# Prompt attention of a hybrid decoder step: one visit for each unit instead of two, with its pace, its query blocks and its compressed scores moved

## The chip, the core and the metric

The kernel runs on one core of one Trainium2 chip. The metric is the device time of one execution in microseconds (us). TensorE is PE in what follows (PEld is its weight load, which runs beside the matmuls), VectorE is DVE, ScalarE is ACT, GpSimd is POOL, SyncE is SP. Each engine takes its instructions in the order in which the program writes them.

## What is computed

One layer of a decoder for two groups of requests that share the weights: 256 prompt tokens and 8 x 8 sample tokens, 320 columns together.

```python
x = x + 0.5 * swiglu_ffn(rmsnorm(x, ffn1_norm), ffn1_w_in, ffn1_w_out)
h = rmsnorm(x, mix_norm)
z, xbc, dt_raw, q, kv, nsa_g, merge_g = jnp.split(h @ w_in_proj, cuts, axis=-1)
y_ssm, new_conv, new_ssm = mamba_mixer(z, xbc, dt_raw, ...)     # conv, chunked scan, gated norm
o, new_win = nsa_fn(q, gates, paged_rows, win_rows, compress_kv, bias_tab)
mix = (gm[..., :D_MODEL] * (y_ssm @ w_branch_ssm) + gm[..., D_MODEL:] * (o @ w_branch_attn)) @ w_out
x = x + mix
x = x + 0.5 * swiglu_ffn(rmsnorm(x, ffn2_norm), ffn2_w_in, ffn2_w_out)
```

`nsa_fn` is attention in three branches for every head: compressed (one key for each 32 tokens), selected blocks, and a sliding window, each with a softmax of its own; the three are added with a sigmoid gate each. For the prompt, 256 tokens have only four selectable blocks, so that the selected branch and the window branch are both plain causal attention with their own keys and values.

## The kernel before, in words

**The dense stream.** All weights go through `dense` (L328 to L354). A weight block of 128x1024 is split into a high and a low part (`wh` on ACT, L317; `wl` on DVE, L326), and each of its eight slices makes three matmuls over the 320 columns, L345, L346 and L347. These three are called a k-tile here. There are 1928 of them in the program, and they are written in a fixed order: first feed-forward, input projection (q, k, v, then 24 tiles of `xbc`, each with a short convolution, `conv_unit`), merge gates, z, two branch outputs, output, second feed-forward.

**The work beside it.** Everything else is written as Python generators that the class `Sched` steps through. After each k-tile `S.tick()` adds half of `S.rate` to a credit, and for each whole credit one generator goes on to its next `yield`. What it issues up to there, on whatever engine, stands in the program between two k-tiles. Such a step is called a visit. Two generators in the queue take turns. `RATE` holds the rates of the stages, and `pace(i)` sets them: `RATE[3]` is that of the prompt attention. At 1.5 there are 0.75 visits for each k-tile.

**Prompt attention** (`prompt_attn`) has 32 units: four query blocks `qc` of 64 tokens, and in each of them eight units `u` (two heads on 128 partitions). Beside it, taking turns, runs the chain `values_tok`, `new_keys`, `cmp_sample` (the sample tokens' compressed branch), and then that chain is done. A unit goes through

- `scores` (L1317 on PE into a bank of tag `sc`, sum with bias and minimum on DVE L1323, exponential on ACT L1326),
- `norm` (reciprocal on DVE L1334, scaling on POOL L1337),
- `transposes` (L1349 on PE into a bank of tag `pt`, copied to `pT` by ACT L1350),
- `values` (L1366 on PE into the bank `po`, of which there is one; after the eighth unit ACT copies it out, L1370).

Once in a query block, `build` writes the next block of queries (POOL L1281), `cmp_a` computes its compressed scores (L1288 on PE, nine small DVE instructions and one of ACT), and `cmp_b` turns them (L1310 on PE into `pt` banks, copied by ACT L1311). Tags `sc` and `pt` have two PSUM banks each, shared with the other chain.

The convolution's tanh (L1246) is on ACT between these, and waits for three DVE instructions (L1245). `conv_unit` puts them off by four k-tiles.

Of the kernel before, what the change touches and what calls it, by code (L numbers as in the profile page):

```python
# [112 lines left out]
W0, W1, W2, W3, WS, EB = 3, 3, 6, 1, 4, 2  # L113
XBC_RUN = [i for q in range(4) for i in (4 * q, 4 * q + 1, 4 * q + 2, 4 * q + 3, 16 + q, 20 + q)]
PROJ_RUN = [12] + list(range(12)) + [17, 18, 19, 20, 13, 14, 15, 16] + [PROJ_X + i for i in XBC_RUN] + [PROJ_M + i for i in range(16)] + [PROJ_Z + i for i in range(16)]
RATE = (0.59, 1.2, 0.9, 1.5, 0.88, 0.57, 1.0)


IDLE = "idle"
# [48 lines left out]
def chain(*gens):  # L168
    for x in gens:
        yield from x  # L170
# [21 lines left out]
def wait(n):  # L192
    for _ in range(n):
        yield
# [3 lines left out]
def step_kernel(ctx, tc, I, O):  # L198
    nc = tc.nc
    pe, v, a, g, sp = nc.tensor, nc.vector, nc.scalar, nc.gpsimd, nc.sync  # L200
# [10 lines left out]
    def bank(tag, shape=(128, 512)):  # L211
        bufs = dict(pd=3, sc=2, pt=2, po=1)[tag]
        t = ps.tile([128, 512], F32, tag=tag, bufs=bufs, name=f"ps_{tag}")[: shape[0], : int(np.prod(shape[1:]))]
        if len(shape) == 3:
            t = t.rearrange("p (a b) -> p a b", a=shape[1])
        elif len(shape) == 4:
            t = t.rearrange("p (a b c) -> p a b c", a=shape[1], b=shape[2])
        return t
# [4 lines left out]
    pt = cp.tile([1, 128], I32, name="pt")  # L223
# [16 lines left out]
    def flat(t):  # L240
        return t.rearrange("p a b -> p (a b)")
# [562 lines left out]
    S.add(cs)  # L804
    S.rate = RATE[0]
    sq = Squares(8)
# [43 lines left out]
    kTp = pp.tile([128, 2, 8], F32, name="kTp")  # L850
# [17 lines left out]
    def bl(o, m, n):  # L868
        return st["blob"][:, o : o + m * n].rearrange("p (a b) -> p a b", a=m)
# [25 lines left out]
    def selector():  # L895
        st["sel"] = pa.tile([128, 12, 128], F32R, name="sel")
        id4 = ident.rearrange("p (x r) -> p x r", x=4)
        for k in range(3):
            gcopy(st["sel"][:, 4 * k : 4 * k + 4, :].rearrange("p x (h d) -> p x h d", h=2),
                  id4[:, :, 2 * k : 2 * k + 2].unsqueeze(3).to_broadcast([128, 4, 2, 64]))  # L900
            yield
# [128 lines left out]

    def values_tok():
        for t in range(2):
            pv = bank("pt")
            for i in range(4):
                pe.transpose(pv[:, 128 * i : 128 * i + 128], vr[:, i, 128 * t : 128 * t + 128], ident)
            a.copy(flat(vtp[:, t]), pv)
            yield
        pv = bank("pt", (128, 256))
        for br in range(2):
            for h2 in range(2):  # L1040
                pe.matmul(pv[64 * br : 64 * br + 64, 128 * h2 : 128 * h2 + 128], vr[:, 2 * br + h2, 256:], ident,
                          start=True, stop=True)
        a.copy(vst, pv)
        yield
# [216 lines left out]
    def prompt_attn():  # L1261
# [3 lines left out]
        qbp = [bl(1024 * i, 8, 128) for i in range(2)]  # L1265
# [4 lines left out]
        def move():  # L1270
            if ready["prep"] and "OT" not in st:
                st["OT"] = hp_.tile([128, 8, NT], F32, tag="OT", name="OT")
            if moves and "OT" in st:
                t = moves.pop()
                a.copy(st["OT"][:, :, t], qn[:, :, t])


        def build(qc):
            for hp in range(2):
                r = slice(64 * hp, 64 * hp + 64)  # L1280
                g.tensor_scalar(qbp[qc % 2][r, :, 64 * hp : 64 * hp + 64], qn[r, 0:8, 64 * qc : 64 * qc + 64], -1.0, 0.0,  # L1281
                                op0=ALU.mult, op1=ALU.add)

        def cmp_a(qc):
            nb, k0 = 2 * (qc + 1), 192 - 64 * qc
            pc = bank("pt", (128, 8, 8))
            for u in range(8):
                pe.matmul(pc[:, u, :nb], qbp[qc % 2][:, u, :], kTp[:, u // 4, :nb], start=True, stop=True)  # L1288
            sc = pl.tile([128, 8, 8], F32, tag="psc", name="psc")
            m = pl.tile([128, 8], F32, tag="psm", name="psm")  # L1290
            s = sc[:, :, :nb]
            bcast = m.unsqueeze(2).to_broadcast([128, 8, nb])
            v.tensor_tensor(s, pc[:, :, :nb], pb[:, :, k0 + 31 :: 32], op=ALU.add)
            v.tensor_reduce(out=m, in_=s, axis=AX.X, op=ALU.min)
            v.tensor_scalar(m, m, 1e20, None, op0=ALU.min)
            v.tensor_tensor(s, s, bcast, op=ALU.subtract)
            a.activation(s, s, AF.Exp, scale=-1.0)
            v.reduce_sum(m, s, axis=AX.X)
            v.tensor_scalar(m, m, 1e-30, None, op0=ALU.max)
            v.reciprocal(m, m)  # L1300
            gq = gtp[:, qc].rearrange("p (u r) -> p u r", r=3)
            v.tensor_tensor(m, m, gq[:, :, 0], op=ALU.mult)
            v.tensor_tensor(s, s, bcast, op=ALU.mult)
            pend["c"] = sc

        def cmp_b(qc, q):
            nb, sc = 2 * (qc + 1), pend["c"]
            tps = bank("pt")
            for i in range(4):
                pe.transpose(tps[:nb, 128 * i : 128 * i + 128], sc[:, 4 * q + i, :nb], ident)  # L1310
            a.copy(flat(pcT[qc % 2][:nb, 4 * q : 4 * q + 4]), tps[:nb])  # L1311

        def scores(i):
            qc, u = divmod(i, 8)
            nk, k0 = 64 * (qc + 1), 192 - 64 * qc
            p = bank("sc", (128, 2, 256))
            pe.matmul(p[:, :, :nk], qbp[qc % 2][:, u, :], knp[:, :, u // 4, :nk], start=True, stop=True)  # L1317
            P = pl.tile([128, 2, 256], F32, tag="pS", bufs=4, name="pS")
            if nk % 128:
                g.memset(P[:, :, nk : nk + 64], 0.0)  # L1320
            m = pl.tile([128, 4], F32, tag="pm", bufs=6, name="pm")
            for br in range(2):
                v.tensor_tensor_reduce(out=P[:, br, :nk], in0=p[:, br, :nk], in1=pb[:, u, k0:256], op0=ALU.add,  # L1323
                                       op1=ALU.min, scale=1.0, scalar=3e38, accum_out=m[:, br : br + 1])
            for br in range(2):
                a.activation(P[:, br, :nk], P[:, br, :nk], AF.Exp, bias=m[:, br : br + 1], scale=-1.0,  # L1326
                             accum_out=m[:, 2 + br : 3 + br])
            pend["s", i] = P, m

        def norm(i):  # L1330
            qc, u = divmod(i, 8)
            nk = 64 * (qc + 1)
            P, m = pend["s", i]
            v.reciprocal(m[:, 2:4], m[:, 2:4])  # L1334
            for br in range(2):
                o = 3 * u + 1 + br
                g.tensor_scalar(P[:, br, :nk], P[:, br, :nk], m[:, 2 + br : 3 + br], gtp[:, qc, o : o + 1], op0=ALU.mult,  # L1337
                                op1=ALU.mult)


        def transposes(i):
            nt = (i // 8 + 2) // 2
            P = pend.pop(("s", i))[0]
            tps = bank("pt")
            pT = pl.tile([128, 4, 128], F32, tag="pT", bufs=2, name="pT")
            for k in range(nt):
                for br in range(2):
                    o = (k * 2 + br) * 128
                    pe.transpose(tps[:, o : o + 128], P[:, br, 128 * k : 128 * k + 128], ident)  # L1349
            a.copy(flat(pT[:, 0 : 2 * nt, :]), tps[:, 0 : 256 * nt])  # L1350
            pend["t", i] = pT
# [20 lines left out]
                    moves.append(slice(64 * qc, 64 * qc + 64))  # L1372

        build(0)
        yield from wait(2)
        cmp_a(0)
        yield from wait(4)
        cmp_b(0, 0)
        cmp_b(0, 1)
        for i in range(4):  # L1380
# [6 lines left out]
        for i in range(32):  # L1387
            qc, u = divmod(i, 8)
            if i + 3 < 32:
                norm(i + 3)  # L1390
            if i + 1 < 32:
                transposes(i + 1)
            if i + 4 < 32:
                scores(i + 4)
            yield
            values(i)
            move()
            if qc < 3:
                if u == 1:
                    build(qc + 1)  # L1400
                elif u == 2:
                    cmp_a(qc + 1)
                elif u == 4:
                    cmp_b(qc + 1, 0)
                    cmp_b(qc + 1, 1)
            yield
        pr_stack.close()
        yield from until("prep")
# [475 lines left out]
    def until(name):  # L1884
        while not ready[name]:
            yield IDLE

    ssq = bank("po", (128, NT))
    def pace(i):
        S.rate = RATE[i]  # L1890
        yield IDLE
# [9 lines left out]
    early = chain(cmp_keys(), bias_, selector(), until("gates"), both(gates_rows(), decays()))  # L1901
    S.rate = RATE[1]
    S.add(chain(early, until("qk"), pace(2), qk_norm(ssq), done("qn"), until("side"), attention()),
# [28 lines left out]
    for i in range(4):  # L1932
# [5 lines left out]
        c, h2 = divmod(i, 2)  # L1938
# [281 lines left out]
```

## Time and profile before

| | us |
|---|---|
| three runs | 1324.02, 1332.32, 1332.83; median 1332.32 |
| the profiled execution | 1327.57 |
| its span, first to last instruction | 1325.9 |
| PE busy in the span | 1262.7 (95%) |
| DVE, ACT, POOL busy | 877.8, 590.7, 372.7 |

The profiled execution is 4.7 us below the median of the three runs, so a difference worked out in the profile is taken from the median. PE's ends are modelled, and a busy PE is not PE at its peak. What a stage costs is read from when its k-tiles start, and from what PE waited for between them.

### The profile page before, as it was taken

The page shows a single profiled execution, that of the slowest core. Times are in us where ns is not written, and L with a number is a line of the kernel's source. Part 1 is how long each engine was busy: PE and PEld are TensorE (multiplying, and loading weights), DVE is VectorE, ACT ScalarE, POOL GpSimd, SP SyncE. Part 2 cuts the span into 40 slices and gives each one's busy share as a digit, 9 for nine tenths or more (in the row PEclk, how much of TensorE's full clock was granted, in tenths as well). Part 3 has the DMA queues.
Part 4 walks back from the last instruction along what each step waited for, and adds up shares of the span by engine and source line. Part 5 has one row for each costly group of instructions (what it writes and reads, how often), then busy time and mean ns, then how long its engine had stood idle before and what let it go on. Part 6 is the DMA issues. An engine that isn't in the chain of part 4 may idle for free.

```text
span 1325.9 us, 28576 instructions
## 1 busy us (share of the span) xinstructions
PE 1262.7 (95%) x10779; PEld 1149.6 (87%) x10779; DVE 877.8 (66%) x1872; ACT 590.7 (45%) x1149; POOL 372.7 (28%) x625
## 2 busy tenths in 40 slices
PE   8999999999999998889998898998989999999998
PEld 8899999999988888777896576776769999999998
DVE  5576666655576577975578687778667766666542
ACT  4344444454444334446664343456563343333322
POOL 2232321323100335655435353444420010000000
PEclk9899999999989999999999899999999999999999
DMA  8466665677653445511177775899973534444553
GB/s 278 153 210 216 209 200 190 219 227 216 212 163 125 142 138 206 191 66 63 49 223 244 220 222 174 315 357 313 343 274 115 178 130 146 156 146 157 152 162 92
DMA packets 98501, 251.67 MB, mean 190 GB/s; under 512 B 14649, under 2 KB 41274, under 8 KB 96410
## 3 DMA queue, kind: packets, MB, share of 16 engines
q1 hardware_dynamic: 81370, 198.24, 45.5%
q0 software_dynamic: 16992, 51.61, 11.7%
q8 instruction: 85, 1.39, 0.4%
q14 instruction: 54, 0.43, 0.1%
HBM read 235.07 MB, written 23.10 MB: 195 GB/s over the span
## 4 chain that ended last, share of the span: by engine, by line
PE 57%; DVE 17%; issue 12%; ACT 5%; DMA 4%; POOL 3%; SPq 1%; POOLq 1%; DVEq 0%; ACTq 0%
PE ps_pd L345 15%; PE ps_pd L346 13%; PE ps_pd L347 13%; DVE wl L326 4%; ACT wh L317 2%; DVE cvo L1245 2%; DMA out_ssmS<-h 2%; PE ps_sc L1478 2%; PE ps_po L1518 1%; PE ps_sc L713 1%; PE ps_sc L714 1%; PE ps_sc L723 1%; PE ps_pt L1504 1%; PE ps_po L1366 1%; PE ps_sc L1317 1%
## 5 line engine op out<-in xcount | busy, mean ns | idle before, releaser
L345 PE MATMUL ps_pd<-hh,wh 128*128 128x320 f32 x1320 | 440.7, 334 | 2.9 <-ACT hh L261 1.8
L326 DVE TENSOR_TENSOR wl<-wraw,wh 128x1024 fp32r<-128x1024 f32 (+1 forms) x245 | 305.4, 1248 | 184.9 <-ACT wh L317 179.4
L346 PE MATMUL ps_pd<-hl,wh 128*128 128x320 f32 x1320 | 413.4, 313 | 1.3 <-DVE hl L454 1.1
L347 PE MATMUL ps_pd<-hh,wl 128*128 128x320 f32 x1320 | 413.5, 313 | 1.1 <-DVE wl L326 1.1
L317 ACT CAST wh<-wraw 128x1024 fp32r<-128x1024 f32 (+1 forms) x245 | 252.2, 1031 | 139.8 <-PE ps_pd L346 100.7
L345 PEld LDWEIGHTS ps_pd<-hh,wh 128*128 128x128 f32 x1320 | 252.9, 192 | 22.0 <-issue 11.3
L346 PEld LDWEIGHTS ps_pd<-hl,wh 128*128 128x128 f32 x1320 | 253.4, 192 | 9.6 <-issue 4.8
L347 PEld LDWEIGHTS ps_pd<-hh,wl 128*128 128x128 f32 x1320 | 252.6, 191 | 1.6 <-DVE wl L326 1.6
L345 PE MATMUL ps_pd<-ah,wh 128*128 128x320 f32 x352 | 109.4, 311 | 0.0
L347 PE MATMUL ps_pd<-ah,wl 128*128 128x320 f32 x352 | 108.9, 309 | 0.0
L580 DVE TENSOR_TENSOR pgl<-pg,pgh 128x512 fp32r<-128x512 f32 x128 | 82.5, 685 | 29.7 <-ACT pgh L573 28.8
L346 PE MATMUL ps_pd<-al,wh 128*128 128x320 f32 x320 | 98.8, 309 | 0.0
L568 POOL DMA_DIRECT2D pg<-in_cache x136 | 74.2, 546 | 83.4 <-DVE pgl L580 42.3
L238 POOL TENSOR_SCALAR ah<-ff 128x320 fp32r<-128x320 f32 x44 | 20.1, 456 | 272.5 <-DVE ff L482 272.5
L573 ACT CAST pgh<-pg 128x512 fp32r<-128x512 f32 x128 | 72.7, 617 | 9.7 <-PE ps_sc L714 9.0
L477 ACT ACTIVATE sg<-sg 128x320 f32<-128x320 f32 x44 | 20.8, 472 | 125.7 <-DVE sg L476 125.7
L1431 POOL DMA_DIRECT2D KV<-in_cache x102 | 54.9, 539 | 76.4 <-PE ps_po L1518 43.2
L713 PE MATMUL ps_sc<-pgh,w1h 128*128 128x256 f32 x256 | 68.5, 288 | 1.0 <-ACT pgh L573 1.0
L714 PE MATMUL ps_sc<-pgh,w1l 128*128 128x256 f32 x256 | 68.3, 289 | 0.0
L345 PEld LDWEIGHTS ps_pd<-ah,wh 128*128 128x128 f32 x352 | 66.2, 188 | 0.4
L347 PEld LDWEIGHTS ps_pd<-ah,wl 128*128 128x128 f32 x352 | 66.1, 188 | 0.0
L346 PEld LDWEIGHTS ps_pd<-al,wh 128*128 128x128 f32 x320 | 60.2, 188 | 0.0
(476 smaller groups left out, 2207.9 us busy)
## 6 DMA issues: line engine op xcount, KB each, us to landing
wraw<-in_wproj SPq DMA_DIRECT2D x77, 512.0 KB
KV<-in_cache POOLq DMA_DIRECT2D x102, 256.0 KB, 6.1
wraw<-in_w1in SPq DMA_DIRECT2D x44, 512.0 KB
wraw<-in_w2in SPq DMA_DIRECT2D x44, 512.0 KB
pg<-in_cache POOLq DMA_DIRECT2D x136, 128.0 KB, 4.0
pg<-in_cache SPq DMA_DIRECT2D x120, 128.0 KB
wraw<-in_w1out SPq DMA_DIRECT2D x16, 512.0 KB
h<-in_ssm SPq DMA_DIRECT2D x32, 256.0 KB
```

Of the source, the lines that this page charges most:

```text
L317: a.copy(h[:, :n], st["raw"][i][:, :n])
L326: v.tensor_tensor(l[:, :n], st["raw"].pop(i)[:, :n], st["hl"][i][0][:, :n], op=ALU.subtract)
L345: pe.matmul(out, wh[:, s], xh[:, kk, :], start=kk == 0, stop=False)
L346: pe.matmul(out, wh[:, s], xl[:, kk, :], start=False, stop=False)
L347: pe.matmul(out, wl[:, s], xh[:, kk, :], start=False, stop=kk == K - 1)
L568: e.dma_start(page(s, half)[:, i, :], I["cache"][ds(r, 1), :, 256 * c : 256 * c + 256].rearrange("o p f -> p (o f)"))
L573: a.copy(h[:, 8 * half : 8 * half + 8, :], page(s, half)[:, :, 64 * q : 64 * q + 64])
L580: v.tensor_tensor(l[:, 8 * half : 8 * half + 8, :], page(s, half)[:, :, 64 * q : 64 * q + 64], h[:, 8 * half : 8 * half + 8, :], op=ALU.su ...
L713: pe.matmul(ph, wh[:, j, :], h[:, :, j, :], start=q + j == 0, stop=False)
L714: pe.matmul(ph, wl[:, j, :], h[:, :, j, :], start=False, stop=False)
L1245: v.scalar_tensor_tensor(o, pr[:, k : k + 344], w(k), o, op0=ALU.mult, op1=ALU.add)
L1431: e.dma_start(t[:, j, :], I["cache"][ds(r, 1), :, 512:1024].rearrange("o p f -> p (o f)"))
```

## The change

In a unit, `values` now follows `scores` in the same visit, where a `yield` stood between them. The rate goes from 1.5 to 1.05. The compressed scores are made by four matmuls with 32 stationary columns each, in place of one with 128. `build` comes one unit sooner, `cmp_a` one unit later, and the two halves of `cmp_b` in two units. The first block waits three visits after `build` (two before) and three after `cmp_a` (four before). The second of the three banks in `values_tok` is of tag `sc` (`pt` before).

```diff
-RATE = (0.59, 1.2, 0.9, 1.5, 0.88, 0.57, 1.0)
+RATE = (0.59, 1.2, 0.9, 1.05, 0.88, 0.57, 1.0)
...
         for t in range(2):
-            pv = bank("pt")
+            pv = bank("sc" if t else "pt")
...
             for u in range(8):
-                pe.matmul(pc[:, u, :nb], qbp[qc % 2][:, u, :], kTp[:, u // 4, :nb], start=True, stop=True)
+                for c in range(4):
+                    o = slice(32 * c, 32 * c + 32)
+                    pe.matmul(pc[o, u, :nb], qbp[qc % 2][:, u, o], kTp[:, u // 4, :nb], start=True, stop=True)
...
         build(0)
-        yield from wait(2)
+        yield from wait(3)
         cmp_a(0)
-        yield from wait(4)
+        yield from wait(3)
...
                 scores(i + 4)
-            yield
             values(i)
             move()
             if qc < 3:
-                if u == 1:
+                if u == 0:
                     build(qc + 1)
-                elif u == 2:
+                elif u == 3:
                     cmp_a(qc + 1)
-                elif u == 4:
-                    cmp_b(qc + 1, 0)
-                    cmp_b(qc + 1, 1)
+                elif u in (5, 6):
+                    cmp_b(qc + 1, u - 5)
             yield
```

Two lines are added, so that L1310 before is L1312 after, and so on to the end of `prompt_attn`; L1288 is L1290.

On PE, in the third query block, a unit stood like this before: transposes of one unit, scores of a later one, a k-tile, then values of an earlier one.

```order
L1349 MATMUL ps_pt<-con,pS 128x128 x2
L1317 MATMUL ps_sc<-knp,blob 128x2x192
L345 MATMUL ps_pd<-hh,wh 128x320
L346 MATMUL ps_pd<-hl,wh 128x320
L347 MATMUL ps_pd<-hh,wl 128x320
L1366 MATMUL ps_po<-pT,vtp 64x64 x4
L1366 MATMUL ps_po<-blob,vcp 64x64 x2
```

Now the unit at which the last compressed scores are made stands like this, with them at its end.

```order
L1351 MATMUL ps_pt<-con,pS 128x128 x4
L1319 MATMUL ps_sc<-knp,blob 128x2x192
L1368 MATMUL ps_po<-pT,vtp 64x64 x8
L1368 MATMUL ps_po<-blob,vcp 64x64 x2
L1290 MATMUL ps_pt<-kTp,blob 32x8 x32
```

The k-tiles between transposes and values are gone, and the eight matmuls of L1288 (one row of `128x8 x8` before) are 32 over 32 partitions.

On PE in `values_tok`, ahead of all units, one piece of the difference:

```order
 L346 MATMUL ps_pd<-hl,wh 128x320
 L347 MATMUL ps_pd<-hh,wl 128x320
-L1035 MATMUL ps_pt<-con,vr 128x128 x4
+L1035 MATMUL ps_sc<-con,vr 128x128 x4
 L345 MATMUL ps_pd<-hh,wh 128x320
 L346 MATMUL ps_pd<-hl,wh 128x320
```

Only the bank's tag moved there; the next user of the `pt` tag is L1041, two k-tiles later.

On ACT, where the first query block ends, before (the copy of `po` is L1370, `cvt` is the convolution's tanh):

```order
L1246 ACTIVATE cvt<-cvo 128x344
L1350 COPY pT<-ps_pt 128x256
L1326 ACTIVATE pS,pm<-pS,pm 128x128 x2
L1234 COPY pr_4944<-ps_pd 128x256
L1235 COPY pr_4944<-ps_pd 128x8x8
L317 CAST wh<-wraw 128x1024
L1370 COPY qn<-ps_po 128x8x64
L1246 ACTIVATE cvt<-cvo 128x344
```

And now:

```order
L1246 ACTIVATE cvt<-cvo 128x344
L1352 COPY pT<-ps_pt 128x256
L1328 ACTIVATE pS,pm<-pS,pm 128x128 x2
L1313 COPY blob<-ps_pt 4x512
L1234 COPY pr_4944<-ps_pd 128x256
L1235 COPY pr_4944<-ps_pd 128x8x8
L317 CAST wh<-wraw 128x1024
L1352 COPY pT<-ps_pt 128x256
L1328 ACTIVATE pS,pm<-pS,pm 128x128 x2
L1372 COPY qn<-ps_po 128x8x64
L1246 ACTIVATE cvt<-cvo 128x344
```

Between two tanhs ACT now has a second unit's copy and exponentials, and half of the copies of `cmp_b`, ahead of the copy of `po`.

## Rows read from the trace of the kernel before

**Rows 1.** Windows of four stretches: us, busy us (and instructions) by engine, PEclk, DMA.

```profile
475.17:504.91 29.74, 26.27 (x228) 24.39 (x227) 22.90 (x55) 9.83 (x23) 18.38 (x32) 0.94 0.45 158
504.91:523.78 18.87, 16.04 (x245) 14.94 (x244) 13.96 (x39) 8.14 (x26) 8.55 (x15) 0.91 0.50 178
523.78:596.55 72.77, 61.92 (x574) 54.73 (x572) 61.13 (x170) 34.45 (x114) 46.14 (x85) 0.95 0.39 143
596.55:660.35 63.80, 62.09 (x640) 50.78 (x638) 36.19 (x125) 41.17 (x115) 28.90 (x68) 1.00 0.18 59
```

**Rows 2.** Waits of PE, 475 to 665: total us, times, longest.

```profile
PE ps_po L1366 <- ACT qn L1370: 3.6, 1, 3.6
PE ps_pt L1288 <- POOL blob L1281: 2.9, 2, 2.0
PE ps_pt L1310 <- ACT pT L1350: 2.9, 1, 2.9
PE ps_pt L1035 <- DVE kTp L1127: 2.6, 1, 2.6
PE ps_sc L1317 <- DVE pm L1323: 1.9, 1, 1.9
PE ps_pt L1349 <- POOL pS L1337: 1.7, 1, 1.7
...
PE ps_pt L1349 <- ACT blob L1311: 0.7, 1, 0.7
```

**Rows 3.** Windows of two short stretches, columns as above.

```profile
492.69:496.10 3.41, 3.41 (x18) 2.80 (x17) 2.27 (x5) 0.70 (x2) 0.95 (x2) 0.50 0.50 172
...
571.20:574.60 3.40, 3.40 (x23) 3.24 (x22) 2.44 (x6) 0.06 (x1) 1.41 (x3) 0.50 0.46 154
```

**Rows 4.** Timeline of PE: the matmuls of compressed scores, and two others with few columns.

```profile
496.91 2.04 PE L1053 MATMUL ps_sc<-ksm,qbs 128*64 128x8 f32 x64
...
593.15 1.10 PE L1212 MATMUL ps_sc<-kcv,cpT 128*32 128x64 f32 x64
...
616.48 1.95 PE L1288 MATMUL ps_pt<-kTp,blob 128*128 128x8 f32 x16
```

**Rows 5.** Timeline of PE around one visit of values.

```profile
544.26 0.31 PE L347 MATMUL ps_pd<-hh,wl 128*128 128x320 f32 x1
544.50 0.45 PE L1366 MATMUL ps_po<-pT,vtp 128*64 128x64 f32 x8
544.78 0.29 PE L1366 MATMUL ps_po<-blob,vcp 128*64 128x64 f32 x4
545.00 0.42 PE L345 MATMUL ps_pd<-hh,wh 128*128 128x320 f32 x1
...
545.54 0.31 PE L345 MATMUL ps_pd<-hh,wh 128*128 128x320 f32 x1
```

**Rows 6.** Timeline where the transposed keys of the compressed branch are copied.

```profile
491.18 0.16 DVE L1127 COPY kTp<-ps_pt 128x16 f32<-128x16 f32 x1
...
491.40 0.66 PE L1035 MATMUL ps_pt<-con,vr 128*128 128x128 f32 x4 [2.58 <-DVE kTp L1127]
```

**Rows 7.** Waits of ACT for DVE, 475 to 665: total us, times, longest.

```profile
ACT cvt L1246 <- DVE cvo L1245: 36.2, 14, 5.7
...
ACT cvt L1246 <- DVE pm L1334: 22.8, 8, 4.0
```

**Rows 8.** Timeline from the transposes of unit 8 to its values.

```profile
561.79 0.38 PE L1349 MATMUL ps_pt<-con,pS 128*128 128x128 f32 x2
...
567.44 0.49 ACT L1246 ACTIVATE cvt<-cvo 128x344 f32<-128x344 f32 x1 [4.70 <-DVE cvo L1245]
567.83 0.35 ACT L1350 COPY pT<-ps_pt 128x256 f32<-128x256 f32 x1
...
570.39 0.59 ACT L1370 COPY qn<-ps_po 128x512 f32<-128x512 f32 x1
...
571.04 0.60 PE L1366 MATMUL ps_po<-pT,vtp 128*64 128x64 f32 x8 [3.58 <-ACT qn L1370]
```

## The prediction

> **What bounds the kernel now.** I read the whole first: PE is busy 95% of the span, so time is gained only where PE stands, runs slowly, or has less to do. The change touches nothing ahead of `values_tok`, and behind the prompt attention every stage keeps its instructions. So next come the windows around the 32 units [rows 1], in which the reader should compare PE with DVE. From 596 to 660 PE is busy 62.1 of 63.8 us: 19 units stand there at 2.7 k-tiles each, and PE itself is the bound. From 524 to 597, with 13 units and the sample chain, PE is busy 61.9 of 72.8 us, and DVE 61.1, or 84%. Here PE waits for things that come from DVE or through it. The waits of PE [rows 2] name them: in these 190 us PE waited 18 us in pieces of up to 3.6 us, for POOL's query block, for copies by ACT, for DVE. Last, short windows [rows 3]: four stretches of 3.4 us each (two are shown) had a granted clock of 0.50, which is 1.2 of 2.4 GHz. Each began within about 3 us after PE had stood for 0.9 to 3.6 us; after the two waits for the query block the compressed scores, matmuls of a few columns, came in between.
>
> Pace: a unit took two visits. At rate 1.5 that is 2.7 k-tiles, and 5.3 while the other chain takes every second visit. Now it takes one visit at 1.05: 1.9 k-tiles, and 3.8 beside the other chain. That chain itself is visited every 3.8 k-tiles, not every 2.7, and by the order its last matmuls (L1212) stand 42 k-tiles later. So 25 units run at 3.8, seven at 1.9, and the last values stand 3 k-tiles later than before. The change doesn't shorten the program; it evens out the load.
>
> **The change part by part** (against the profiled 1327.6 us).
>
> *a. Compressed scores on quarters.* L1288 takes 1.95 us for 16 passes (8 matmuls of two passes) [rows 4]. The new form is 64 passes with 32 stationary columns. The nearest row is L1212, with the same 128x32 weights and more columns: 64 passes in 1.10 us. Four times 0.85 saves 3.4 us, all on PE's path. The other bound is L1053, 64 passes with 64 stationary columns and 8 moving, 2.04 us: then it costs 0.4 us. I take L1212, since its weights have the form that is added.
>
> A rule speaks against this part. The Trainium skill, "TensorEngine Tiling (Array Packing)", section "Instruction Overhead", says that each matmul has an overhead of about 60 cycles, and that no tiling factor should be taken where a dimension is already small. An estimate from that page is 64 passes of 25 ns, 1.6 us, so that four would save 1.4 us and not 3.4. L1212's 17 ns a pass is under this price, so the trace doesn't bear it out for this form; with 2 to 8 moving columns no run has shown it.
>
> *b. Queries a unit sooner, scores a unit later.* L1288 waited for POOL's block twice, 0.9 and 2.0 us, 2.9 in all [rows 2]. Now three units, 11 k-tiles, lie between `build` and `cmp_a` instead of one, and three visits for the first block. Both waits go: -2.9. Next late there is nothing: the keys are older.
>
> *c. The second bank of `values_tok`.* L1035 waited 2.6 us for the copy of the transposed keys [rows 2, 6], so it was ready at 488.8. On an `sc` bank it goes at once, but two k-tiles later L1041 takes the bank that this copy must free, at 491.3. With L1035 at 0.7 us and two k-tiles at 0.44 it gets there at 490.4, and waits 0.9 to 1.1. That is -1.5; bounds 0 and -2.6.
>
> *d. Halves of `cmp_b` apart.* L1310's second half waited 2.9 us for a `pt` bank, and the transposes behind it 0.7 [rows 2]. With one half in a visit, each finds its bank freed a unit ago: -3.6. What ACT does late comes under *h*.
>
> *e. One visit instead of two.* From L347 at 544.26 to L345 at 545.54 are 1.28 us: four dense matmuls at 0.145 (0.58), and 0.70 for the visit, of which its own matmuls, 544.50 to 545.00, are 0.50 [rows 5]. So 0.2 us go into and out of the dense stream. 32 visits fewer save at most 6.4. The way out stays, now behind the same matmuls; I take half, -3.2; bounds 0 and -6.4.
>
> *f. Clock.* Four stretches of 3.4 us at half clock lost 6.8 us in all [rows 3]. They follow waits that *b* and *c* end or cut, and the wait for `po`, which stays. I take half, -3.4; bounds 0 and -6.8.
>
> *g. Other waits* (3.6 us for `po`, L1317's 1.9, L1349's 1.7) [rows 2] I leave as they are. `po` can be waited for at three ends of a query block, once it was: bounds -5 and +7.
>
> *h. What comes back.* Two readings give the same size. First DVE: 15 units instead of 13 end in those 70 k-tiles, a part of the sample chain leaves them, and without PE's waits 72.8 us would become 62, which is DVE's own 61.1 [rows 1]. An engine in order, itself waiting for ACT and POOL, doesn't reach 100%; at 90% it holds the stretch at 68 us, 6 above 62. Second the copy: a unit's `pT` must be there for its values. Before, 8 k-tiles lay between (4 in the fast part); now 3.8 (1.9). ACT stands in order behind the convolution's tanh, which waited for DVE 22 times for 59 us [rows 7]. Unit 8's transposes ended at 562.2, and its copy came at 567.8 [rows 8], 5.7 us later; 3.8 k-tiles at this stretch's 1.04 us are 4.0. Such a copy would now hold PE for 1.7 us. Four such make 6 us. I take +6; bounds 0 and +15.
>
> Instructions and DMAs are otherwise the same; SP's and POOL's queues keep their DMAs. All later stages stand 3 or 4 k-tiles later against the weights: 0 to +1.8, taken at 0.
>
> Sum: -3.4 - 2.9 - 1.5 - 3.6 - 3.2 - 3.4 + 6 = -12.0. The profiled execution would take 1315.6, and the median of 1332.3 would become **1320**.
>
> **The rivals.**
>
> *PE sets the pace.* DVE is busy only 36.2 of 63.8 us in the second window [rows 1]; if what it falls behind in the first is made up there, *h* is nothing. With all of *e*, three quarters of *f*, and half of the wait for `po`, it is -3.4 - 2.9 - 1.5 - 3.6 - 6.4 - 5.1 - 1.8 = -24.7: 1308. For it: banks and split weights allow PE some k-tiles of lead. Against it: ACT waits for DVE in each convolution unit [rows 7], however long DVE's average rests.
>
> *The wait changes its name.* DVE holds 524 to 597 at its 72.8 us, and whatever is taken from PE's waits there turns into waits for scores, copies and `wl`. Then only what lies outside counts: *c*, the first of *b* (0.9), and half of *a* (1.7), -4.1: 1328. For it: 84% already. Against it: DVE's work for the sample chain moves out of this stretch.
>
> *Slower: late copies, once for each convolution.* Values now stand behind scores and transposes of their own visit, so that a late `pT` or `po` holds all dense work. There are 17 convolutions in the 138 k-tiles of the units. If each held PE for 1.7 us as worked out in *h*, it would be +29 in place of +6, and the clock would gain nothing either (*f*): -18 + 3.4 + 29 = +14.4, so 1347. It turns positive from 0.9 us for each. Against it: none of the waits in [rows 2] is one of values for `pT`, though in the fast part only 4 k-tiles lay between.
>
> **How the numbers follow.** The forecast gets 0.45, PE's pace 0.25, the changed name 0.22, the slower case 0.08. Runs of one kernel here are 0.66% apart, so 1% (13 us, under 1319 or over 1346) is about what can be told from no change. Faster by over 1%: all of the first rival and under half of the forecast's spread, 0.45. Within 1%: 0.47. Slower: 0.08, the last rival. The range is 1306 to 1333: it takes in the first rival and most of the second, and leaves out the slower case and the far ends.
>
> **What the profile after would show.** *a*: L1290 64 passes in about 1.1 us. *b*: no wait of PE for POOL's block. *c*: L1041 waiting about 1 us for the keys' copy. *d*: nothing over 0.5 us at L1312. *f*: two of the four slow stretches left. *h*: DVE at or over 90% where units and sample chain stand together, and new waits of L1368 for `pT`. I'd be wrong if DVE rested there and PE didn't wait (then 1308), or if L1368's waits came to over 18 us (then slower).

## The result and the profile after

The change made the kernel slower by 6 to 7 us: median 1336.56 us of 20 runs (1330.01 to 1344.56) against 1330.70 of 20 runs before (1323.80 to 1333.83), a ratio of 1.0053 with an interval of 1.0038 to 1.0069. The forecast was 1320 (12 under the 1332.3 of the first three runs), its range ended at 1333. The profiled execution has a span of 1331.8 us, 5.9 more than before, and a mean granted clock of 0.978 (0.982 before).

Where did it go? Both kernels have the same 1928 k-tiles, whose start times cut both spans alike. Cut at k-tiles 722, 884 and 1260, they give the 32 units, and then the later stages that have side work (scan, z tiles, sample attention). Two rows for each kernel, the units and the later stages; first before, columns as in [rows 1].

```profile
487.26:662.00 174.74, 155.88 (x1605) 134.92 (x1604) 124.39 (x360) 91.15 (x270) 98.16 (x191) 0.96 0.33 119
662.00:1023.79 361.79, 335.21 (x3523) 260.76 (x3522) 271.56 (x732) 172.81 (x382) 142.93 (x186) 0.98 0.76 255
```

The same two windows of the kernel after:

```profile
483.69:656.26 172.57, 152.62 (x1791) 129.59 (x1790) 122.51 (x361) 91.36 (x272) 96.26 (x191) 0.94 0.35 121
656.26:1026.26 370.00, 339.27 (x3530) 264.74 (x3529) 273.76 (x731) 172.06 (x379) 143.91 (x186) 0.97 0.76 249
```

In these two profiles the units gained 2.2 us, not 12, and the later stages, whose instructions are the same, lost 8.2. One profile of each is weak evidence for that. Up to k-tile 700 the two programs are the same, and yet the profiles are 3.6 us apart there (475.17 and 471.61 us). Four profiles have the later stages in the order and at the place of before, and these took 361.8 us (before), 362.9 (quarters), 365.8 and 369.4 (the kernel without its one visit, profiled twice); the last of them:

```profile
656.81:1026.24 369.43, 342.60 (x3523) 265.11 (x3522) 271.93 (x732) 172.82 (x382) 142.93 (x186) 0.96 0.75 249
```

So where the time goes has to be settled by timed runs, further below. Cut by the k-tiles of [rows 1] the four stretches from `values_tok` to the last units are, after:

```profile
471.61:495.53 23.92, 22.66 (x212) 21.48 (x211) 18.61 (x42) 8.11 (x18) 13.65 (x26) 1.00 0.38 130
495.53:513.88 18.35, 13.23 (x141) 12.31 (x140) 14.68 (x36) 5.27 (x14) 8.61 (x15) 0.91 0.66 220
513.88:591.15 77.27, 65.71 (x781) 56.71 (x779) 59.89 (x187) 39.95 (x135) 43.69 (x87) 0.89 0.41 146
591.15:655.27 64.12, 62.11 (x744) 49.66 (x741) 38.92 (x126) 40.69 (x112) 34.93 (x75) 1.00 0.17 59
```

Against [rows 1] the first is 5.8 us shorter (the bank of `values_tok`, one stretch at half clock fewer, and the first compressed scores, which now stand in the second stretch), and the third is 4.5 us longer, though DVE is busy 78% of it and not 84%. Its PEclk fell from 0.95 to 0.89. PE's waits in all four stretches (total, times, longest), to be laid beside [rows 2]:

```profile
PE ps_pt L1351 <- ACT pT L1352: 5.0, 2, 3.8
PE ps_sc L1319 <- DVE pm L1325: 4.9, 2, 3.4
PE ps_pt L1312 <- DVE psc L1305: 4.6, 1, 4.6
PE ps_po L1368 <- ACT pT L1352: 3.4, 4, 1.3
PE ps_pt L1041 <- DVE kTp L1127: 1.3, 1, 1.3
PE ps_pt L1290 <- POOL blob L1281: 0.5, 1, 0.5
```

The waits that the prediction struck out are gone: for the query block 0.5 us are left of 2.9, for the bank behind `values_tok` 1.3. Others stand in their place, and the sum is 20 us where it was 19: the transposes wait for the copy `pT`, the first `cmp_b` for its scores. The new compressed scores were cheap. The timeline of PE, at full clock:

```profile
611.29 0.72 PE L1290 MATMUL ps_pt<-kTp,blob 128*32 128x8 f32 x64
```

The clock is part of the story. The profile after has about 59 us at 1.2 GHz in all, before 50. Among them are four stretches in the units (20.4 us, where [rows 3] stood for four of 3.4) and three between 810 and 849 us, from k-tile 1053 to a little past 1088, where before had none. Two of each:

```profile
510.39:513.80 3.41, 3.41 (x16) 3.15 (x15) 2.72 (x6) 1.04 (x4) 0.21 (x2) 0.50 0.67 214
524.00:530.80 6.80, 5.62 (x46) 5.16 (x47) 4.09 (x18) 4.09 (x14) 3.22 (x10) 0.50 0.79 295
...
834.60:838.00 3.40, 3.40 (x16) 3.40 (x14) 3.40 (x7) 1.73 (x3) 2.60 (x5) 0.50 0.86 258
844.85:848.26 3.41, 3.41 (x14) 3.41 (x14) 2.96 (x17) 0.56 (x1) 0.00 (x0) 0.50 1.00 381
```

One profile can't carry this alone, but every timed run beside an experiment, and all 20 of the change, list their span and mean granted clock (of the 20 runs before beside the change only the time is listed). In a stretch at half clock the dense matmuls run at about half their pace (after, one started every 0.27 us at 545.5 us, every 0.15 at 501). If all of that were lost, span x (1 - clock) would be what a run lost to the clock, and the rest its time at full clock. The means: before lost 26.9 us and has a rest of 1302.5 (127 runs beside all experiments); after lost 34.0 and has a rest of 1302.2 (20 runs). Read so, all of the slowdown would be granted clock.

That reading is an upper bound. Among the 127 runs of the kernel before, a run with one more us lost by this formula took only 0.46 us longer, and among the 20 runs of the change 0.64: presumably a part of what a slow stretch loses would have been waited for anyhow, or is made up later. At these slopes the 7.1 us of lost clock would account for 3 to 5 of the 6 to 7 us. **By these figures half or more of the slowdown is granted clock; that it is all of it is not shown.** Nor is it shown what brought the clock down.

### The profile page after: what moved, and what is told of

Read it like the earlier page. It is cut to its first block, busy times and chain, and to the rows that moved or that the text cites. A ratio compares the mean times of both kernels' runs of the same rounds, so it can differ in the third digit from the quotient of the medians.

```text
span 1331.8 us, 28953 instructions
## 1 busy us (share of the span) xinstructions
PE 1263.5 (95%) x10971; PEld 1147.4 (86%) x10971; DVE 877.4 (66%) x1872; ACT 591.1 (44%) x1151; POOL 370.6 (28%) x625
## 5 line engine op out<-in xcount | busy, mean ns | idle before, releaser
L345 PE MATMUL ps_pd<-hh,wh 128*128 128x320 f32 x1320 | 433.8, 329 | 3.1 <-ACT hh L261 1.8
L326 DVE TENSOR_TENSOR wl<-wraw,wh 128x1024 fp32r<-128x1024 f32 (+1 forms) x245 | 303.8, 1242 | 197.3 <-ACT wh L317 192.9
```

Source lines behind the costliest of these rows:

```text
L326: v.tensor_tensor(l[:, :n], st["raw"].pop(i)[:, :n], st["hl"][i][0][:, :n], op=ALU.subtract)
L345: pe.matmul(out, wh[:, s], xh[:, kk, :], start=kk == 0, stop=False)
```

## The experiments

Each kernel was timed in five rounds beside the kernel before. The table is in the order of the text; its last two columns are worked out as above, so "lost to the clock" is an upper bound. Before has 26.9 and 1302.5.

| run | ratio to before, interval | clock | lost to the clock, us | rest, us |
|---|---|---|---|---|
| quarters | 0.9996, 0.9976 to 1.0017 | 0.980 | 26.5 | 1301.5 |
| one_visit | 1.0106, 1.0076 to 1.0135 | 0.975 | 33.8 | 1310.0 |
| moves_two_visits | 0.9978, 0.9956 to 1.0000 | 0.979 | 28.0 | 1299.1 |
| moves_two_visits_2 | 0.9989, 0.9966 to 1.0013 | 0.978 | 29.3 | 1299.0 |
| later_stages_4_ktiles | 1.0090, 1.0065 to 1.0116 | 0.976 | 31.9 | 1309.2 |
| later_stages_9_ktiles | 1.0081, 1.0053 to 1.0109 | 0.980 | 27.2 | 1313.3 |
| one_visit_rate_107 | 1.0003, 0.9979 to 1.0028 | 0.978 | 29.1 | 1300.1 |
| one_visit_rate_108 | 1.0106, 1.0077 to 1.0135 | 0.973 | 36.2 | 1307.1 |
| one_visit_rate_109 | 1.0102, 1.0073 to 1.0132 | 0.975 | 34.2 | 1308.7 |
| only_scan_starts_later | 1.0020, 1.0003 to 1.0038 | 0.977 | 30.3 | 1302.6 |
| only_sample_attn_later | 0.9986, 0.9970 to 1.0002 | 0.980 | 26.2 | 1302.4 |
| only_scan_ends_later | 1.0082, 1.0052 to 1.0113 | 0.977 | 31.0 | 1309.3 |
| after_scan_end_back | 0.9999, 0.9975 to 1.0022 | 0.978 | 29.5 | 1300.5 |
| kv_after_states | 1.0048, 1.0027 to 1.0069 | 0.974 | 34.4 | 1301.6 |
| filled_wait | 1.0069, 1.0043 to 1.0095 | 0.973 | 36.6 | 1301.6 |
| z_work_behind_scan | 1.0043, 1.0021 to 1.0064 | 0.975 | 33.1 | 1301.4 |
| z_work_partly_behind | 1.0044, 1.0022 to 1.0066 | 0.974 | 34.6 | 1300.1 |
| z_work_behind_kv_after | 1.0036, 1.0017 to 1.0056 | 0.977 | 30.9 | 1302.5 |

### The parts of the change

**quarters**: the kernel before with the four matmuls of 32 stationary columns in `cmp_a`, nothing else.

> Only the compressed scores on four quarters of the stationary columns; every k-tile, visit and wait stands as in the kernel before. Term a of the prediction says -3.4 us (four blocks, 0.85 us each), if PE's path is where it counts. If PE merely waits longer for DVE at the next unit, 0. If the 64 passes cost as L1053's, +1.6. The ratio is then between 0.997 and 1.001; the visit of 64 passes itself should show about 1.1 us in the profile (2.0 by the other bound).

No gain can be told: -0.5 us with an interval of -3.2 to +2.3, so that -3.4 is just outside it. PE waited for the query block 2.1 us (2.9 before) and then for what it had once been early enough for; two of the waits of this run:

```profile
PE ps_pt L1312 <- ACT pT L1352: 4.1, 1, 4.1
...
PE ps_pt L1290 <- DVE ic L1159: 1.8, 1, 1.8
```

**one_visit**: the kernel before with

```diff
-RATE = (0.59, 1.2, 0.9, 1.5, 0.88, 0.57, 1.0)
+RATE = (0.59, 1.2, 0.9, 1.05, 0.88, 0.57, 1.0)
...
                 scores(i + 4)
-            yield
             values(i)
```

> Only the one visit for each unit and the rate of 1.05; quarters, bank, query blocks and the places of the compressed scores stay as before. Theory 1 (the later stages, which now stand 3 to 4 k-tiles later against the weights, lose about 6 us): units 0 to -2 us against before, later stages +5 to +8, so 1.003 to 1.006. Theory 2 (the loss is in the units: waits renamed, more half-clock stretches; the later stages only differ by chance): units +4 to +8, later stages within 2 us, so again 1.003 to 1.006. The two are told apart by the stage in which the time goes, not by the whole.

It is 14 us slower, more than either theory gave. In its profile (its slowest run, 1350.8 us) units and later stages both lost against before, 4.6 and 13.5 us, so that the two theories aren't told apart:

```profile
489.26:668.65 179.39, 159.82 (x1598) 137.09 (x1597) 121.68 (x361) 91.71 (x272) 96.63 (x191) 0.92 0.32 116
668.65:1043.93 375.28, 340.46 (x3530) 264.41 (x3529) 274.20 (x731) 172.19 (x379) 143.87 (x186) 0.97 0.75 246
```

The change, which has the remaining parts too, loses only half as much.

**moves_two_visits**: the change with those two edits undone.

> Everything else of the change (quarters, second bank, query blocks a unit sooner, compressed scores a unit later, their halves apart), but with the two visits for each unit and the rate of 1.5 of the kernel before. The later stages stand against the weights as before. Terms a to d of the prediction say -3.4 - 2.9 - 1.5 - 3.6 = -11.4 us, with some of the clock more. If waits only change their name, -2 to -4. Both theories of the loss put it in the one visit, so both say below before, -3 us or more (ratio 0.998 or less).

**moves_two_visits_2**: the same kernel once more.

> Again the change without its one visit and its rate (quarters, bank, query blocks, halves), as a version that could beat both kernels: 0.996 to 1.000 if the first run's -2.5 us holds.

-2.9 and -1.5 us: parts *a* to *d* together are worth about 2 us, where the prediction summed 11.4. It beats the changed kernel; whether it beats the kernel before, two intervals that touch and cross 1 do not settle.

### The place of the later stages

**later_stages_4_ktiles**: the kernel before, its units untouched, with

```diff
-        yield from chain(pace(3), prompt_attn(), pace(4), ssd(), pace(5), sample_attn(), pace(6), merge_prep())
+        yield from chain(pace(3), prompt_attn(), pace(4), wait(2), ssd(), pace(5), sample_attn(), pace(6), merge_prep())
```

> The kernel before with two empty visits between the prompt attention and the scan, so that the scan, the sample attention and all behind them stand 4 k-tiles later against the weights, as the change puts them; the units are untouched. Theory 1 (the place of the later stages costs): +5 to +8 us, ratio 1.004 to 1.006. Theory 2 (the loss is in the units): 0 within 1.3 us.

Theory 1, and more than it asked: +12 us for empty visits alone (interval 8.6 to 15.4). Its profile has the units at 175.05 us (before 174.74) and the later stages, k-tiles 884 to 1260, at

```profile
662.93:1037.49 374.56, 340.34 (x3531) 265.02 (x3529) 271.91 (x731) 171.69 (x379) 144.59 (x187) 0.97 0.74 246
```

**later_stages_9_ktiles**: `wait(4)` instead of `wait(2)`.

> The kernel before with four empty visits between the prompt attention and the scan: all later stages stand 9 k-tiles later. If each k-tile later costs about 3 us (less work of the z tiles is left to cover the scan's end), +25, ratio 1.019. If 4 k-tiles fell on one bad place (a step), +5 to +14, 1.004 to 1.010.

+11 us: not 3 us for each k-tile, a step. None of it is clock by the table (27.2 us lost, before 26.9).

**one_visit_rate_107**: the changed kernel at 1.07, which puts the later stages back.

> The changed kernel with a rate of 1.07 in place of 1.05 in the prompt attention: its last values and all later stages then stand at the same k-tiles as in the kernel before, give or take one. Theory 1 (the place of the later stages costs 7 to 12 us): 2 to 5 us under before, ratio 0.996 to 0.999. Theory 2 (one visit costs in the units, wherever the later stages stand): 1.003 to 1.006 as the changed kernel.

+0.4 us, interval -2.8 to +3.7. So 0.02 of rate, which puts the later stages three k-tiles earlier, is worth about 7 us. Its windows as above, units and later stages:

```profile
483.76:657.47 173.71, 152.98 (x1797) 129.35 (x1796) 124.07 (x360) 90.93 (x272) 97.37 (x191) 0.94 0.34 120
657.47:1019.56 362.09, 335.74 (x3523) 260.30 (x3522) 267.88 (x732) 173.07 (x382) 142.33 (x186) 0.99 0.75 254
```

**one_visit_rate_109** and **one_visit_rate_108**: the same with 1.09 and 1.08, later stages three and one k-tile earlier than before.

> The changed kernel with a rate of 1.09: the later stages stand 3 k-tiles earlier than in the kernel before. If each k-tile costs about 3 us in either direction, 9 us under the run at 1.07, ratio to before about 0.990. If it is a step that the kernel before just misses, the same as the run at 1.07 within 1.5 us.

> The changed kernel at a rate of 1.08: the later stages stand one k-tile earlier than in the kernel before. If the good place is one of several k-tiles, as at 1.07, within 3 us of before (0.999 to 1.002). If each k-tile away from it costs, +4 to +6 (1.003 to 1.005).

Both 14 us slower, which no theory had given. In the profile at 1.08 the units take 179.57 us and the later stages 369.08: 4.8 and 7.3 us more than before. The units of one_visit and of the run at 1.09 took as long (179.4 and 179.5). Why is not shown, and it was not followed further; it isn't the place found below, where both runs are as quick as before (k-tiles 1048 to 1088 in 30.6 and 30.9 us).

```profile
485.58:665.15 179.57, 155.82 (x1820) 130.81 (x1818) 124.45 (x363) 91.45 (x273) 99.74 (x193) 0.94 0.35 120
665.15:1034.23 369.08, 335.43 (x3500) 262.58 (x3500) 270.93 (x729) 172.74 (x381) 141.98 (x184) 0.97 0.75 248
```

### Which of the later stages

**only_scan_starts_later**: the kernel before with `wait(2)` ahead of `ssd()` as above, and a rate of 0.90 in place of 0.88 for the scan, so that its end is within a k-tile of where it was.

> The kernel before with two empty visits ahead of the scan, and the scan's rate raised from 0.88 to 0.90: the scan starts 4 k-tiles later, and its end (last transposes L1847) and the sample attention stand where they stood before. If the scan's start or its place against the convolutions' end costs, +12 as with everything 4 k-tiles later. If the scan's end among the z tiles, or the sample attention's place, costs, within 2 us of before.

**only_sample_attn_later**: the kernel before with `ssd(), wait(2), pace(5), sample_attn()`.

> The kernel before with the two empty visits behind the scan: the scan stands as before, the sample attention and all behind it 4 k-tiles later. If the scan's end among the z tiles costs (1048 to 1088, where every trace with later stages shows 6.8 to 10.2 us at half clock and those without 0 to 2.5), within 2 us of before, ratio 0.999 to 1.002. If the sample attention's place costs, +8 to +12.

+2.7 us and -1.9 us: neither is the 12. What is left is the scan's end, which stands among the z tiles.

The scan goes through four quarters. In each, for the sample tokens, PE multiplies the loaded states (L1819), POOL scales them (L1821), PE makes their update (L1824, L1825), DVE adds it (L1826); at the end DVE writes `ys` (L1835), which PE transposes (L1847). The 16 z tiles stand at k-tiles 1016 to 1144; each is gated on DVE (L2002, L2003), and each four get a norm (sums L396 on PE, roots on DVE, L410 on PE). In the fourth quarter the last L1847 stands at k-tile 1072 in the kernel before and at 1076 after. The end was then moved in both directions by the scan's rate, with the scan's start left where it was. This shifts the scan's last quarters and the sample attention behind it along with the end.

**only_scan_ends_later**: the kernel before, scan's rate 0.865.

> The kernel before with the scan's rate lowered from 0.88 to 0.865: the scan starts as before, its last transposes stand 4 k-tiles later, the sample attention 3. Theory 1c: +7 to +12, ratio 1.005 to 1.009. If start and end must both be late for the loss, within 3 us of before.

**after_scan_end_back**: the changed kernel, scan's rate 0.896.

> The changed kernel with the scan's rate raised from 0.88 to 0.896: the prompt attention and the scan's start stand as in the changed kernel, the scan's last transposes at k-tile 1072 and the sample attention at 1090, as in the kernel before. Theory 1c (the scan's end among the z tiles, 4 k-tiles later, loses the 7 us): as the run at 1.07, within 3 us of before (0.998 to 1.002), with a mean clock of 0.978. If the one visit or the scan's start loses them: 1.004 to 1.006, clock 0.975.

Both came as theory 1c says: +11 us in the kernel before, and the whole loss of the changed kernel gone. The sample attention's place cost nothing by itself. So the place is the scan's end, or its last quarters with it. Windows of k-tiles 1048 to 1088, in the order before, after, only_scan_ends_later, after_scan_end_back (one fence for each kernel):

```profile
814.69:845.65 30.96, 27.18 (x166) 22.99 (x164) 24.39 (x56) 8.06 (x14) 12.01 (x16) 1.00 0.75 257
```

```profile
799.95:844.61 44.66, 34.74 (x203) 28.46 (x201) 32.46 (x66) 9.56 (x17) 17.26 (x19) 0.92 0.61 197
```

```profile
810.12:855.24 45.12, 35.71 (x203) 29.79 (x201) 32.44 (x62) 10.08 (x17) 17.69 (x19) 0.89 0.60 196
```

```profile
810.13:845.99 35.86, 29.86 (x179) 23.92 (x177) 29.11 (x63) 9.57 (x17) 14.88 (x19) 1.00 0.72 242
```

The late ones hold 24 to 37 more matmul records, work that the others did ahead of this window, so 14 us are not the loss. K-tiles 884 to 1088 together took 183.7, 188.4, 193.3 and 182.6 us in the same order, so the loss up to there is about 5 and 10. In the windows shown PE stood 9 to 10 us and not 4 to 6, and PEclk is 0.92 and 0.89 and not 1.00. PE's waits in the window, before:

```profile
PE ps_pt L396 <- DVE ncol L401: 1.2, 1, 1.2
PE ps_po L1819 <- DMA h<-in_ssm: 1.2, 1, 1.2
PE ps_sc L1702 <- DVE h L1826: 1.0, 1, 1.0
PE ps_sc L1824 <- DVE h L1826: 0.4, 1, 0.4
```

And after:

```profile
PE ps_sc L1824 <- DVE h L1826: 3.4, 1, 3.4
PE ps_pt L396 <- DVE ncol L401: 2.7, 1, 2.7
PE ps_pt L1847 <- DVE ys L1835: 2.4, 1, 2.4
PE ps_po L1819 <- DMA h<-in_ssm: 1.4, 1, 1.4
```

The same window in only_scan_ends_later has the same two waits on the scan:

```profile
PE ps_sc L1824 <- DVE h L1826: 3.2, 1, 3.2
PE ps_pt L1847 <- DVE ys L1835: 3.2, 1, 3.2
```

### What at that place costs

Two possible causes can be read from the timelines. First, in DVE's order, after has the gate of a z tile (L2002, L2003) and the split of a weight (L326) ahead of the scan's first sums, and PE's L1824 needs the bank that these free:

```profile
803.61 0.47 DVE L2002 SCALAR_TENSOR_TENSOR zth<-zth,ps_pd 128x320 f32<-128x320 f32 x1
...
807.65 2.07 DVE L326 TENSOR_TENSOR wl<-wraw,wh 128x1024 fp32r<-128x1024 f32 x1
809.64 1.27 DVE L1826 TENSOR_TENSOR h<-h,ps_sc 128x512 f32<-128x512 f32 x2
```

while before has the sums first:

```profile
815.88 1.27 DVE L1826 TENSOR_TENSOR h<-h,ps_sc 128x512 f32<-128x512 f32 x2
817.07 0.47 DVE L2002 SCALAR_TENSOR_TENSOR zth<-zth,ps_pd 128x320 f32<-128x320 f32 x1
```

Second, POOL. The scaling of the last two states (L1821) stands behind the first load of the sample attention's KV, and that load waits until the stored `St` has landed (after, timeline of POOL). Before, it stood 5.2 us there, for DVE's L2002.

```profile
829.49 1.16 POOL L1431 DMA_DIRECT2D KV<-in_cache  x2 [9.34 <-DMA out_ssmP<-St]
830.66 2.08 POOL L1821 TENSOR_TENSOR h<-h,cdb 128x512 f32<-128x512 f32 x2
```

**kv_after_states**: the changed kernel with the first load one visit later.

```diff
-            load_kv(i, (g, sp, g, sp))
-            yield
+            if i != 1:
+                yield
+            load_kv(i, (g, sp, g, sp))
+        yield
```

> The changed kernel, in which the first early load of the sample attention's KV is issued together with the second, one visit of its chain later, so that POOL scales the last two states (L1821) before it waits for the stored St. The number of visits and the place of everything on PE stay as in the changed kernel. Theory 1a (the later stages lose because POOL's last two scalings stand behind that load, 9.3 us in the changed kernel, so that DVE's sum, ys and PE's last transposes come late): the 2.4 us wait of L1847 goes, and what follows it, -3 to -6 us against the changed kernel, ratio to before 1.000 to 1.003. Theory 1b (the collision is one of DVE's work for the z groups with the last quarter of the scan; the load is only the last of several late things): within 1.3 us of the changed kernel, 1.004 to 1.006.

The wait of L1847 went, the time did not: theory 1a is out (whether 1b holds, the z runs below ask). In its profile k-tiles 1048 to 1088 took 6.6 us less than in the changed kernel, and 1088 to 1260 then 8.6 more than its 181.65 (1026.26 - 844.61). The four profiles with the order of before took 178.1 to 182.7 there, so this loss is clear of their spread; what makes it is open:

```profile
806.10:844.15 38.05, 34.01 (x202) 28.04 (x200) 32.15 (x66) 9.66 (x17) 18.41 (x19) 0.91 0.58 189
844.15:1034.38 190.23, 173.55 (x2373) 127.97 (x2372) 129.80 (x473) 96.20 (x214) 60.27 (x113) 0.96 0.79 277
```

**filled_wait**: the changed kernel with, ahead of the last L1847,

```diff
+                for _ in range(10 if q == 3 else 0):
+                    pe.matmul(p[:, 0:128], ones, ones, start=True, stop=True)
```

> The changed kernel with ten further matmuls of 128x128 ahead of the scan's last transposes (L1847), where PE waits 2.4 us for ys in the changed kernel; they take 0.27 us each, 2.7 us, and write nothing that is read. If PE's standing there brings the stretch at half clock behind it, the stretch goes, and the time falls by up to 3 us against the changed kernel (1.002 to 1.004 to before), with a mean clock nearer 0.977. If the clock there has another cause, the same or up to 1 us more (1.005 to 1.006), clock 0.974 to 0.975.

The wait of L1847 went here too, but PEclk in the window of k-tiles 1048 to 1088 is 0.86, and the time is no better. Other waits were longer in this profile (4.7 us at L1824, 4.2 at L396, where after has 3.4 and 2.7). Filling this one wait did not bring the clock back.

```profile
801.07:847.65 46.58, 37.66 (x223) 31.49 (x221) 32.67 (x66) 10.36 (x17) 17.50 (x19) 0.86 0.60 192
```

**z_work_behind_scan**, **z_work_partly_behind**, **z_work_behind_kv_after**: the changed kernel with `e` = 4, with 2, and with 4 together with the later load.

```diff
-        S.defer(1, gated)
-        S.defer(2, lambda: sq.square(y))
-        S.defer(3, lambda: sq.gather(v))
+        e = 4 if i == 3 else 0
+        S.defer(1 + e, gated)
+        S.defer(2 + e, lambda: sq.square(y))
+        S.defer(3 + e, lambda: sq.gather(v))
         if i % 4 == 3:
-            S.defer(4, sq.sums)
-            group_norm(i // 4, sq)
+            S.defer(4 + e, sq.sums)
+            group_norm(i // 4, sq, e)
```

(`group_norm` adds `e` to its own two steps.)

> The changed kernel, with DVE's and PE's small work for the fourth z tile and its group's norm put off by 8 k-tiles, so that it stands behind the last quarter's state sums (L1826) and ys (L1835) in DVE's order; the scan, the weights and all else stay. If that work ahead of the sums is what costs, PE's wait of 3.4 us at L1824 and the 2.4 us at L1847 go, and the time falls by 3 to 7 us: 1.000 to 1.003. If the place costs in another way (the clock, the transfers): 1.004 to 1.006.

> As the run beside it, put off by 4 k-tiles only: the tile's two gates stand behind the first pair of sums, the norm's twelve small instructions still ahead of the last pair. If the first pair's place is what costs (L1824's 3.4 us), the same as the run beside it; if the norm ahead of ys costs (L1847), only half of it: 1.002 to 1.005.

> The first run's edit together with the later KV load, so that neither DVE's z work nor POOL's wait for the stored St stands ahead of the last sums. If the two waits were each other's cover (each edit alone gives its gain back at the other), this one shows both: 0.998 to 1.001. If not, as the first run.

About 1.0043, 1.0044 and 1.0036 against 1.0053 of the change: 1 to 2 us, inside the intervals. With `e` = 4 L1824 still waited 2.4 us, and a new wait of 2.8 stood at L410 for the norm. With the later load added, L1847's wait was gone and L1824's still 2.4. So taking away L1847's wait doesn't bring the time back, and the wait at L1824 was only shortened, never taken away: it stays a rival. That the scan's end (or its last quarters) costs at this place is shown; which of its collisions does is open. So is the share of the clock. From after to after_scan_end_back, 4.5 us of lost clock and 1.7 of rest went. But where the same end was put late in the kernel before, most of the loss is rest: only_scan_ends_later has 4.1 us more of lost clock and 6.8 more of rest, later_stages_9_ktiles 0.3 and 10.8.

## Why the prediction was wrong, point by point

**Two steps failed.** The first is that the terms *a* to *d* were added up at the size of the waits, -11.4, with *f* at -3.4 on top. Time for time they gave about 2 us together (moves_two_visits and moves_two_visits_2: -2.9 and -1.5), since PE went on to stand for the next late thing. With the later stages in their old place, the whole change gave +0.4 us (one_visit_rate_107) and not -12. The second is the sentence "All later stages stand 3 or 4 k-tiles later against the weights: 0 to +1.8, taken at 0", which gave no reason for either number. By one_visit_rate_107 and after_scan_end_back it is about +7: the prediction did not look at what the scan's end would stand beside. Had only one of them failed, the time would have lain inside the range (about 1327, with the second alone) or at its end (about 1333, with the first); the second makes the change slower instead of worth nothing.

*a*, -3.4: on PE it saves even more (0.72 us for 64 passes against 1.95, so 1.2 and not 0.85 each). In time no gain was told (quarters), and PE's waits over the units add up to 20 us in its profile, 19 before. The rule of the Trainium skill that was weighed there, "TensorEngine Tiling (Array Packing)", section "Instruction Overhead", gave an estimate of 1.6 us for the 64 passes; the trace has 0.72, so that the estimate is too high for this form. That section's advice on small dimensions is about the dimension that is split; here the 128 stationary columns were split, and the few moving columns were left whole. *b* and *c* did on PE what they should: 0.5 us are left of 2.9, and L1041 waits 1.3, where 0.9 to 1.1 was worked out. *d* was wrong for the first block: `cmp_b` waits 4.6 us at L1312, not for a bank but for the chain of small DVE instructions that `cmp_a` starts: the same 11 k-tiles lie between them, but DVE takes the chain up later. Before, it began as soon as the scores were there; after, 5.6 us behind them (PE ended them at 500.2 us), since one convolution's L1245 and a split weight (L326) now stand ahead of it in DVE's order. PE got there 1.4 us sooner besides (5.0 us behind the scores, 6.4 before, when a stretch at half clock lay between). The chain's first instruction, before and after:

```profile
505.09 0.18 DVE L1293 TENSOR_TENSOR psc<-ps_pt,pb 128x16 f32<-128x16 f32 x1 [0.49 <-PE ps_pt L1288]
```

```profile
505.81 0.17 DVE L1295 TENSOR_TENSOR psc<-ps_pt,pb 128x16 f32<-128x16 f32 x1
```

Together *a* to *d* gave 1.5 to 2.9 us and not 11.4. The rival "the wait changes its name" foresaw this outcome, with its 4.1, but not for its reason: DVE, which was to hold the long stretch at 84%, is busy 78% of it.

*e* and *h*, -3.2 + 6: the one visit with the later stages in place, one_visit_rate_107 against moves_two_visits, costs about 2.6 us (0.0014 to 0.0025 in ratio, though the intervals overlap). The sum of 2.8 fits, but that may be luck: nothing at all is within the intervals too, and of its two readings DVE at 90% was wrong (78%). PE's waits are for single late instructions (the copy `pT` 3.8 us, the minimum `pm` 3.4 us).

*f*, -3.4, has the wrong sign. I took it that fewer waits mean fewer slow stretches, but the waits had only moved. The loss to the clock, by the formula, rose by 7.1 us over all runs, in the profile by 3.4 us in the units (20.4 us at half clock against 13.6) 5.1 in the three stretches at the scan's end, and about 4 over the whole. *g* was inside its bounds: the wait for `po` did not come, and 3.4 us for `pT` did.

So -12 becomes: *a* to *d* about -2, one visit about +2.6, later stages about +7: +7.6, where 5.9 (medians) to 7.0 (ratio) were measured. These terms are differences between the same runs, so their sum checks little; only the last is borne out by other runs (after_scan_end_back). The rival that ended on the slower side had the wrong mechanism: L1368 waited 3.4 us for `pT` in all, not 1.7 for each of 17 convolutions. What would make the prediction wrong was looked for in the units only.

## What to carry to other kernels

In a program whose side work is laid between the weights by rates, a change of one stage's length moves every later stage against the weights, and that is an edit of its own: price it by what then stands side by side, or undo it with a rate, before the stage's own gain is judged. Time the pure shift (empty visits) as a control. A rate moves all that it paces: 0.01 and 0.02 more than the good one cost 14 us here. A wait that is struck out on PE is worth its size only if the next thing is early. Where stretches at half clock follow waits, work out span x (1 - clock) for many runs, and check against the spread of one kernel's runs how much of it is time (here about half).

## What the runs showed of the hardware that was not expected

- The mean granted clock of one core shifts with the order of the same instructions: from 0.978 (after_scan_end_back, one_visit_rate_107) to 0.973 (one_visit_rate_108), which differ from the change in a rate alone. By the formula that is 29 to 36 us of 1330, and runs of one kernel differ by 2 to 8 us in it (one standard deviation). No rule from single waits to slow stretches was found: filling a wait of 2.4 us did not raise it (0.973, 0.975 without).
- A us of clock lost by the formula went with 0.46 us of time over 127 runs of the kernel before, and with 0.64 over 20 runs of the change.
- 64 passes with 32 stationary and 8 moving columns took 0.72 us, 11 ns each, at full clock.
